# An encoder layer on one core: in the w_down products, weight pieces, adding DMAs, stored sums and x issued at other places

## The chip, the core and the metric

The kernel runs on one core of one Trainium2 chip. The time is device microseconds of that core for one launch. The kernel before takes 2227.09 us (median of three runs, 2224.58 to 2228.4). The profile comes from one further execution, and a kernel's changes are worked out in the times of that execution.

## What is computed

The input is x of 512 tokens by 2048 channels in float32. The layer is

```python
h = rmsnorm(x, attn_norm_w[l]);  proj = h @ w_in[l]      # attention heads and gated linear attention
x = x + concatenate([attn_out, gla_out], axis=-1) @ w_out[l]
h = rmsnorm(x, ffn_norm_w[l])
x = x + (silu(h @ w_gate[l]) * (h @ w_up[l])) @ w_down[l]   # FFN_HIDDEN = 5632
return rmsnorm(x, final_norm_w)
```

The change concerns the last product, with w_down (5632 by 2048).

## The kernel before

The float32 products are made of products of split operands: an operand is split into a rounded part (hi) and what rounding left (lo), and for w_down the products hi\*hi, hi\*lo and lo\*hi are added in PSUM. The large products of the feed-forward part use a seven-product scheme for 2 by 2 blocks (Strassen's, in Winograd's form), so the weights of a block need sums first, then splitting.

The order of the work is written out by hand: each engine (PE for matmuls, ACT and DVE for elementwise work, POOL and SP as issuers of DMAs) gets its instructions in the order in which the Python code records them, and works them off in that order. Buffers are slots: `s4` has 20 slots of 4 KB a partition (tiles named b), `s2` has 62 of 2 KB (tiles named a). A slot is handed out again as soon as the code has put it back; the instruction that then writes it waits on the chip for the last reader.

The product with w_down is done in three parts: four small jobs (`evac_down`), then `Down.run`, then four more jobs and a tail. `Down.run` (L1658) is where the change lies. It works through 64 **pieces**, numbered 0 to 63 here; a piece is one pair of w_down blocks (two row blocks of 128, 512 columns) times one prepared pair of activations, and takes 42 matmuls (L1591, L1592, L1593, three for each half of each of seven products). The pieces form ten **runs**, each the sum over some pairs into seven PSUM banks for one of the four column blocks c:

| run | column block | pieces | what happens at its end |
|---|---|---|---|
| 0, 1, 2 | 0, 1, 2 | 0-5, 6-11, 12-17 | the seven sums are stored in DRAM (`md`, L1614) |
| 3 | 3 | 18-28 | stored (L1614) |
| 4, 5 | 2, 1 | 29-33, 34-38 | added in DRAM to those stored (L1612) |
| 6 | 0 | 39-48 | combined into the result and added to x |
| 7, 8, 9 | 1, 2, 3 | 49-53, 54-58, 59-63 | combined and added to x |

Runs 6 to 9 are the "summed" ones: they begin with the stored sums of the earlier runs. `fetch` (L1555) reads the seven tiles of `md` back into `s2` slots through SP's queue (L1560), and `preload` (L1562) copies each into its PSUM bank on ACT (L1564). A bank is taken by the preload as soon as the run before has read it, so at the last piece of a run ACT has a preload after every evacuation of a bank (L1609 where the run before is stored, L1627 and L1635 where it is combined).

For one piece these steps are needed. SP loads the raw blocks (L1114, 512 KB). DVE makes the sums (`sums`: L1130, L1131, L1132). Then `split` gives hi copies on ACT and lo differences on DVE: in most runs for the raw blocks (128x768) and for the sums (128x1024), L1142 and L1147. In runs 3 and 6, where DVE also prepares activations (`operands`, L1522 to L1538), the lo of the raw blocks is made by `part` (L1474) instead: ACT writes the negative of the raw block rounded (L1481), a DMA issued by POOL adds the raw block to it (L1482, the **adding DMA**), ACT copies the hi (L1483); only the sums are split on ACT and DVE (L1493, L1494). A piece's second matmul, on L1592, is the first that reads the lo of the raw blocks.

In iteration i the code records, ahead of the products of piece i: `sums(i)`, `split(i)`, `sums(i+1)`, `sums(i+2)`, `split(i+1)` and `part(i+2)`; what has been done already is skipped. So while piece i is multiplied, one further piece, i+1, is ready or being made ready. Then come steps of the activations (`make`), the fetch for the next run (in the last piece but one, n = len(part) - 2), and in the second piece of a summed run (n = 1) four loads of x from DRAM by POOL (L1679), which the `residuals` (L1652, on DVE, four of them, two right after a run and two one piece later) add the result to. `combine` (L1618) is the chain of DVE and ACT steps at the end of a summed run (L1621, L1622, L1627, L1635, L1638).

Of the kernel before, what the change touches and what calls it, by code (L numbers as in the profile page):

```python
# [120 lines left out]
def layer(nc, tc, x, attn_norm_w, w_in, rel_table, gw_f, gb_f, gw_b, gb_b, gla_norm_w, w_out,  # L121
# [7 lines left out]
    with tc.manual_schedule(), \  # L129
# [7 lines left out]
        s4 = Slots(p4, N4, 1024, "b")  # L137
# [97 lines left out]
        def run_urgent():  # L235
            while urgent:
                try:
                    next(urgent[0])
                    break
                except StopIteration:  # L240
                    urgent.popleft()
# [911 lines left out]
        class Feed(Blocks):  # L1153
# [183 lines left out]
            def run(self):  # L1337
                for i, (u, q) in enumerate(self.seq):
                    self.load()
                    self.split(i)  # L1340
                    while 2 * q + 1 not in xs:
                        run_urgent()
                    for _ in range((1, 3, 3)[i] if i < 3 else 0):
                        run_urgent()
                    self.sums(i + 1)
                    more = self.sum_steps(i + 2)
                    if q == 0:
                        next(self.making, None)
                    else:
                        next(more, None)  # L1350
                    self.split(i + 1)
                    if i > 3:
                        run_urgent()
                    if q < 3:
                        for _ in more:
                            pass
                        if q < 2:
                            next(self.making, None)
                        self.part(i + 3)
                        if q == 1:  # L1360
                            next(self.making, None)
                    if q == 2 and self.sent:
                        put(self.sent)
                        self.sent = None
                    self.products(i, more)
                    if u == len(self.units) - 1:
                        for p in (2 * q, 2 * q + 1):
                            put(*xs.pop(p).values())
                        down_start(q)
                    if q == self.per - 1:  # L1370
                        self.making = self.combine(u)
                urgent.append(self.last())
# [11 lines left out]
        def g_load(j):  # L1384
            if j < FF // 256 and j not in graw and 2 * j not in gT and j >= state["g"]:
                state["g"] = j + 1
                graw[j] = s4.get(F32, [P, 2, 512])
                sp.dma_start(out=graw[j].t.rearrange("p f t -> p (f t)"), in_=gd[j])

        def g_split(j):  # L1390
            if j in graw:
                r = graw.pop(j)
                for f in (1, 0):
                    hi, lo = s2.get(F32R), s2.get(F32R)
                    if f:
                        act.activation(hi.t, r.t[:, f], AF.Copy, scale=-1.0)
                        dve.scalar_tensor_tensor(lo.t, r.t[:, f], -1.0, hi.f, op0=OP.mult, op1=OP.subtract)
                    else:
                        act.copy(hi.t, r.t[:, f])
                        dve.tensor_tensor(lo.t, r.t[:, f], hi.f, op=OP.subtract)  # L1400
                    gT[2 * j + 1 - f] = (hi, lo)
                put(r)
# [48 lines left out]
        class Down(Blocks):  # L1451
# [206 lines left out]
            def run(self):  # L1658
                for i, (r, q) in enumerate(self.seq):
                    c, part = self.runs[r]  # L1660
                    n = part.index(q)
                    self.load()
                    self.sums(i)
                    self.split(i)
                    self.sums(i + 1)
                    self.sums(i + 2)
                    self.split(i + 1)
                    self.part(i + 2)
                    self.reserve = 11 if r in (4, 5) else 4
                    while q not in self.x:  # L1670
                        self.reserve = 0
                        self.make(1)
                    self.make((r in (3, 6)) + i % 2)
                    if n == len(part) - 2 and r + 1 < len(self.runs) and self.summed(r + 1):
                        self.fetch(r + 1)
                    if self.summed(r) and n == 1:
                        x1[c] = [s2.get() for _ in range(4)]
                        for t in range(4):
                            pool.dma_start(out=x1[c][t].t, in_=xd[4 * c + t])  # L1679
                    self.products(i)  # L1680
                    run_urgent()
                    if r == len(self.runs) - 1:
                        if n == 0:
                            g_load(LAST // 2 - 2)
                        if n == 2:
                            g_split(LAST // 2 - 2)
                            g_load(LAST // 2 - 1)
                            st.until, st.limit = None, 1
                            st.load()
                        if n > 2:  # L1690
                            st.split(later_first + n - 2)
                st.limit, st.big = 3, tail_first
# [142 lines left out]
```

## Time and profile before

| | |
|---|---|
| median of three runs | 2227.09 us |
| the profiled execution | 2224.24 us |
| its span, first to last instruction | 2222.5 us |
| PE busy | 2186.6 us (98%) |
| DVE busy | 1554.6 us (70%) |
| ACT busy | 1201.8 us (54%) |
| POOL busy | 322.5 us (15%) |
| moved by DMA | 373.99 MB, 168 GB/s in the mean |
| `Down.run` on PE | from 1773.96 to 2124.77 us of the span |

Busy PE is not the same as PE at its best: matmuls overlap, and a matmul at the halved clock is just as busy as one at the full clock. What a stage loses is read from its length against its number of matmuls, and from the waits in it.

### The profile page before, as it was taken

Reading aid. Unit: us, or ns where it says so; the run is one execution under the profiler, and the core shown is the slowest. Engines: PE = TensorE matmul, PEld = TensorE weight load, DVE = VectorE, ACT = ScalarE, POOL = GpSimd, SP = SyncE. Lnnn points to the kernel's source line nnn. Section 1 sums busy time; section 2 is a strip of 40 time slices with the busy share of each in tenths; the row PEclk is TensorE's granted clock in tenths of the full one; section 3 lists DMA queues with packets and bytes.
Section 4 is the critical chain, followed back from the end, with each engine's and each line's share of the span. In section 5 each row is a group of like instructions: output and inputs, shape, how many; then the busy total and the mean of one; then the engine's idle time right before and its main releaser. Section 6 shows DMA issues by size and latency. Waiting matters only on the chain.

```text
span 2222.5 us, 33130 instructions
## 1 busy us (share of the span) xinstructions
PE 2186.6 (98%) x12374; PEld 1912.7 (86%) x12374; DVE 1554.6 (70%) x2699; ACT 1201.8 (54%) x2005; POOL 322.5 (15%) x356
## 2 busy tenths in 40 slices
PE   9999999999999999999999999999999999989898
PEld 7888887888888888888888888888888899979886
DVE  4366665745455437888888888888888887868885
ACT  5244444444454346666666666666665656555542
POOL 0000000000000101222222222222222202131000
PEclk9999999999999999999999999999999999999999
DMA  6525625242315325888888888888889857797642
GB/s 207 159 76 146 182 77 147 83 124 61 100 57 187 124 96 128 192 197 204 202 211 196 206 202 198 209 192 214 196 206 212 238 172 225 207 243 215 204 158 76
DMA packets 255457, 373.99 MB, mean 168 GB/s; under 512 B 17951, under 2 KB 179407, under 8 KB 255296
## 3 DMA queue, kind: packets, MB, share of 16 engines
q1 hardware_dynamic: 188768, 252.03, 36.4%
q0 software_dynamic: 65344, 118.80, 27.3%
q8 instruction: 97, 1.59, 0.3%
q10 hardware_dynamic: 1184, 1.06, 0.1%
q14 instruction: 64, 0.52, 0.1%
HBM read 246.58 MB, written 35.19 MB: 127 GB/s over the span
## 4 chain that ended last, share of the span: by engine, by line
PE 92%; DMA 2%; DVE 2%; issue 2%; ACT 1%; POOL 0%; SPq 0%; ACTq 0%; POOLq 0%; DVEq 0%
PE pd L1275 22%; PE pd L1281 11%; PE ps L303 5%; PE ps L304 5%; PE ps L305 5%; PE ps L295 5%; PE ps L297 5%; PE ps L296 5%; PE pe L1275 4%; PE pu L1592 3%; PE pu L1593 3%; PE pu L1591 3%; PE pe L1281 2%; PE ps L529 1%; PE pu L304 1%
## 5 line engine op out<-in xcount | busy, mean ns | idle before, releaser
L1275 PE MATMUL pd<-a,b 128*128 128x512 f32 x2112 | 528.4, 392 | 0.1
L1275 PEld LDWEIGHTS pd<-a,b 128*128 128x128 f32 x2112 | 379.0, 189 | 66.2 <-DVE a L1036 0.5
L1281 PEld LDWEIGHTS pd<-a,b 128*128 128x128 f32 x2112 | 288.5, 190 | 21.5
L1281 PE MATMUL pd<-a,b 128*128 128x256 f32 x2112 | 294.9, 282 | 0.0
L1182 POOL DMA_DIRECT2D b<-b x176 | 209.7, 1248 | 521.6 <-ACT b L1181 393.7
L202 DVE TENSOR_TENSOR a<-b,a 128x512 fp32r<-128x512 f32 x288 | 192.7, 687 | 130.9 <-ACT a L201 130.6
L1220 ACT CAST b<-b 128x1024 fp32r<-128x1024 f32 x176 | 185.4, 1053 | 166.5 <-DVE b L1206 138.5
L1592 PE MATMUL pu<-b,a 128*128 128x256 f32 x896 | 256.6, 286 | 18.5 <-DVE b L1147 9.3
L1591 PE MATMUL pu<-b,a 128*128 128x256 f32 x896 | 256.0, 286 | 2.5 <-ACT pu L1564 2.5
L1593 PE MATMUL pu<-b,a 128*128 128x256 f32 x896 | 255.8, 286 | 0.0
L1221 DVE TENSOR_TENSOR b<-b,b 128x1024 fp32r<-128x1024 f32 x176 | 215.0, 1221 | 50.5 <-ACT b L1220 26.3
L201 ACT CAST a<-b 128x512 fp32r<-128x512 f32 x288 | 169.4, 617 | 48.5 <-PE ps L305 22.3
L1592 PEld LDWEIGHTS pu<-b,a 128*128 128x128 f32 x896 | 174.3, 195 | 20.0 <-DVE b L1147 9.9
L1591 PEld LDWEIGHTS pu<-b,a 128*128 128x128 f32 x896 | 174.3, 195 | 3.1 <-ACT pu L1564 3.1
L1593 PEld LDWEIGHTS pu<-b,a 128*128 128x128 f32 x896 | 174.2, 194 | 0.0
L1303 DVE TENSOR_TENSOR a<-pd,a 128x512 f32<-128x512 f32 x132 | 91.4, 692 | 96.5 <-ACT a L1302 96.5
L1181 ACT ACTIVATE b<-b 128x768 fp32r<-128x768 f32 x176 | 149.4, 849 | 4.7 <-PE ps L305 2.9
L1183 ACT CAST b<-b 128x768 fp32r<-128x768 f32 x176 | 145.5, 827 | 0.6 <-PE ps L305 0.6
L1142 ACT CAST b<-b 128x768 fp32r<-128x768 f32 x86 | 77.0, 941 | 108.9 <-PE pu L1593 104.6
L1302 ACT COPY a<-pd 128x512 f32<-128x512 f32 x132 | 77.6, 588 | 103.0 <-PE pd L1281 103.0
L1203 DVE TENSOR_TENSOR b<-b 128x512 f32<-128x512 f32 x176 | 120.7, 686 | 0.0
L593 ACT CAST b<-ps 128x512 fp32r<-128x512 f32 x64 | 37.6, 587 | 144.8 <-PE ps L529 142.9
(256 smaller groups left out, 4457.4 us busy)
## 6 DMA issues: line engine op xcount, KB each, us to landing
b<-b POOLq DMA_DIRECT2D x197, 384.0 KB, 5.4
b<-in_w_gate_dram SPq DMA_DIRECT2D x88, 512.0 KB, 4.0
b<-in_w_up_dram SPq DMA_DIRECT2D x88, 512.0 KB, 4.5
b<-in_w_down_dram SPq DMA_DIRECT2D x88, 512.0 KB, 5.5
b<-in_w_in_dram SPq DMA_DIRECT2D x48, 512.0 KB, 4.0
b<-in_w_in_dram SPq DMA_DIRECT2D x94, 256.0 KB, 4.3
b<-in_w_out_dram SPq DMA_DIRECT2D x32, 512.0 KB, 4.7
a<-a SPq DMA_DIRECT2D x96, 128.0 KB, 2.4
```

Of the source, the lines that this page charges most:

```text
L201: act.copy(h[2].t, r)
L202: dve.tensor_tensor(h[3].t, r, h[2].f, op=OP.subtract)
L1181: act.activation(lo.t, r, AF.Copy, scale=-1.0)
L1182: pool.dma_start(out=lo.f, in_=r, accum_op=OP.add)
L1183: act.copy(hi.t, r)
L1220: act.copy(hi.t, self.S[i].t)
L1221: dve.tensor_tensor(lo.t, self.S[i].t, hi.f, op=OP.subtract)
L1275: mm(o, wh.t[:, p, k], x_.t.rearrange("p s t -> p (s t)"), start=first and p == 0, stop=False, skip_group_check=True)
L1281: mm(o[:, 256:512], wl.t[:, p, k], x_.t[:, 0], start=False, stop=last and p == 1, skip_group_check=True)
L1591: mm(o, xh[:, t], wh, start=first and not loaded and h == 0, stop=False, skip_group_check=True)
L1592: mm(o, xh[:, t], wl, start=False, stop=False, skip_group_check=True)
L1593: mm(o, xl[:, t], wh, start=False, stop=last, skip_group_check=True)
```

## The change

The products, the sums and the splits stay the same in number and kind; before and after, the order has 11972 rows on PE, 2693 on DVE, 591 on SP and 360 on POOL. What changes is where they are recorded. `part` goes one piece further ahead, to i+3. In the runs that are not 3 or 6, if more than four slots of `s4` are free (more than six in the summed runs), `sums(i+3)` and `split(i+2)` are recorded in iteration i too, so that a second further piece is made ready. With the code's own slot counts this holds in iterations 0-14, 29-35, 51-53, 56-58 and 61-63; it does not hold in 15-17, 36-38, 49, 50, 54, 55, 59 and 60. The fetch moves to the last piece but three, and the loads of x to the last piece but one.

```diff
                     self.sums(i + 1)
                     self.sums(i + 2)
                     self.split(i + 1)
-                    self.part(i + 2)
+                    self.part(i + 3)
+                    if r not in (3, 6) and len(s4.free) > (6 if self.summed(r) else 4):
+                        self.sums(i + 3)
+                        self.split(i + 2)
                     self.reserve = 11 if r in (4, 5) else 4
                     while q not in self.x:
                         self.reserve = 0
                         self.make(1)
                     self.make((r in (3, 6)) + i % 2)
-                    if n == len(part) - 2 and r + 1 < len(self.runs) and self.summed(r + 1):
+                    if n == len(part) - 4 and r + 1 < len(self.runs) and self.summed(r + 1):
                         self.fetch(r + 1)
-                    if self.summed(r) and n == 1:
+                    if self.summed(r) and n == len(part) - 2:
                         x1[c] = [s2.get() for _ in range(4)]
                         for t in range(4):
                             pool.dma_start(out=x1[c][t].t, in_=xd[4 * c + t])
```

The lines below the change stand three further down in the new file (L1679 becomes L1682).

On POOL, at the end of run 5 and the start of run 6, this stood before. The tiles b on the left are the lo of pieces 39, 40, 41, 42 and 43, the md rows are the sums of run 5:

```order
L1482 DMA b_1614_19277<-b_1594_19099 128x768
L1482 DMA b_1620_19348<-b_1600_19162 128x768
L1612 DMA md<-a_1387_19360 128x512
...
L1612 DMA md<-a_1393_19426 128x512
L1482 DMA b_1626_19440<-b_1606_19218 128x768
L1482 DMA b_1633_19516<-b_1612_19274 128x768
L1679 DMA a_1403_19524<-xd 128x512
...
L1679 DMA a_1406_19527<-xd 128x512
L1482 DMA b_1639_19585<-b_1618_19345 128x768
```

And this stands there now:

```order
L1482 DMA b_1608_19235<-b_1594_19036 128x768
L1482 DMA b_1616_19296<-b_1600_19113 128x768
L1482 DMA b_1622_19353<-b_1606_19176 128x768
L1612 DMA md<-a_1387_19365 128x512
...
L1612 DMA md<-a_1393_19431 128x512
L1482 DMA b_1628_19445<-b_1614_19293 128x768
L1482 DMA b_1635_19521<-b_1620_19350 128x768
```

Three adding DMAs (pieces 39, 40, 41) instead of two stand ahead of the seven sums of run 5, and the four loads of x no longer stand between those of pieces 42 and 43.

On DVE, at the end of run 7, this stood before: the lo of piece 54 (L1147), the combine (L1621 and on), two residuals (L1652), the sums and the lo of piece 55 (made from raw block b_1694_20203), two residuals:

```order
L1147 TENSOR_TENSOR b_1710_20389<-b_1688_20145,b_1708_20385 128x768
L1147 TENSOR_TENSOR b_1711_20391<-b_1701_20311,b_1709_20387 128x1024
L1621 TENSOR_TENSOR b_1713_20413<-pu_67_20071,a_1455_20403 128x2x256
...
L1622 TENSOR_TENSOR b_1713_20413<-a_1455_20403,pu_72_20122 128x2x256
L1652 SCALAR_TENSOR_TENSOR a_1444_20205<-b_1713_20413,small,a_1444_20205 128x512
L1652 SCALAR_TENSOR_TENSOR a_1445_20206<-b_1713_20413,small,a_1445_20206 128x512
L1130 TENSOR_TENSOR b_1715_20467<-b_1700_20267 128x512
...
L1147 TENSOR_TENSOR b_1718_20475<-b_1694_20203,b_1716_20471 128x768
L1147 TENSOR_TENSOR b_1719_20477<-b_1707_20381,b_1717_20473 128x1024
L1652 SCALAR_TENSOR_TENSOR a_1446_20207<-b_1714_20453,small,a_1446_20207 128x512
```

And this stands there now:

```order
L1147 TENSOR_TENSOR b_1710_20339<-b_1688_20145,b_1708_20335 128x768
L1147 TENSOR_TENSOR b_1711_20341<-b_1701_20275,b_1709_20337 128x1024
L1130 TENSOR_TENSOR b_1713_20395<-b_1700_20273 128x512
...
L1147 TENSOR_TENSOR b_1716_20403<-b_1694_20203,b_1714_20399 128x768
L1147 TENSOR_TENSOR b_1717_20405<-b_1707_20331,b_1715_20401 128x1024
L1621 TENSOR_TENSOR b_1719_20427<-pu_67_20071,a_1455_20417 128x2x256
...
L1652 SCALAR_TENSOR_TENSOR a_1451_20345<-b_1719_20427,small,a_1451_20345 128x512
L1652 SCALAR_TENSOR_TENSOR a_1452_20346<-b_1719_20427,small,a_1452_20346 128x512
L1652 SCALAR_TENSOR_TENSOR a_1453_20347<-b_1720_20467,small,a_1453_20347 128x512
L1652 SCALAR_TENSOR_TENSOR a_1454_20348<-b_1720_20467,small,a_1454_20348 128x512
L1130 TENSOR_TENSOR b_1721_20525<-b_1706_20287 128x512
```

The sums and lo of piece 55 (again from b_1694_20203) have moved from behind the combine to ahead of it, and the four residuals follow each other with nothing between them.

## The prediction

> **What bounds the kernel now.** The page's chain of work first, then busy time in windows, one for each group of runs of `Down.run`, then single engines where those windows are too long. The chain says that PE sets the end:
>
> ```profile
> PE 92%; DMA 2%; DVE 2%; issue 2%; ACT 1%; POOL 0%; SPq 0%; ACTq 0%; POOLq 0%; DVEq 0%
> ```
>
> The windows are runs 0-2, 3, 4-5, 6, 7, 8 and 9. Look at the length of each and its DMA share (the last column but one):
>
> ```profile
> 1773.96:1864.67 90.71, 90.71 (x757) 90.71 (x756) 73.02 (x106) 47.96 (x68) 13.50 (x23) 1.00 0.58 174
> 1864.67:1921.64 56.97, 55.69 (x464) 55.48 (x463) 47.86 (x85) 38.95 (x59) 12.55 (x19) 1.00 0.95 262
> 1921.64:1972.04 50.40, 50.40 (x422) 50.40 (x421) 36.23 (x49) 25.87 (x36) 9.60 (x13) 1.00 0.71 184
> 1972.04:2035.56 63.52, 53.31 (x422) 52.29 (x421) 41.07 (x72) 38.01 (x58) 16.87 (x23) 0.95 0.97 260
> 2035.56:2066.16 30.60, 27.20 (x213) 26.79 (x211) 25.99 (x37) 14.47 (x20) 2.16 (x4) 0.94 0.56 186
> 2066.16:2096.10 29.94, 26.93 (x212) 26.73 (x211) 25.34 (x36) 14.01 (x19) 2.13 (x4) 0.94 0.56 182
> 2096.10:2124.77 28.67, 25.62 (x213) 25.42 (x212) 23.15 (x35) 14.19 (x20) 2.12 (x4) 1.00 0.81 287
> ```
>
> Runs 0-2 take 90.71/18 = 5.04 us a piece and runs 4-5 take 50.40/10 = 5.04: a piece without waits is 5.04 us. Against that, run 3 (11 pieces) loses 1.53 us, run 6 (10) 13.12, and runs 7, 8, 9 (5 each) 5.40, 4.74 and 3.47. These 28.26 us are all that the change can take away, since the matmuls stay. PE's own waits show where they go:
>
> ```profile
> 1876.31 0.39 PE L1592 MATMUL pu<-b,a 128*128 128x256 f32 x1 [1.28 <-DMA b<-b]
> 1974.44 0.39 PE L1592 MATMUL pu<-b,a 128*128 128x256 f32 x1 [2.12 <-DMA b<-b]
> 1979.40 0.38 PE L1591 MATMUL pu<-b,a 128*128 128x256 f32 x1 [1.23 <-ACT pu L1564]
> 1981.39 0.39 PE L1591 MATMUL pu<-b,a 128*128 128x256 f32 x1 [1.02 <-ACT pu L1564]
> 1993.63 0.58 PE L1592 MATMUL pu<-b,a 128*128 128x256 f32 x1 [5.66 <-DMA b<-b]
> 2044.54 0.39 PE L1592 MATMUL pu<-b,a 128*128 128x256 f32 x1 [3.20 <-DVE b L1147]
> 2074.49 0.39 PE L1592 MATMUL pu<-b,a 128*128 128x256 f32 x1 [3.01 <-DVE b L1147]
> 2104.47 0.39 PE L1592 MATMUL pu<-b,a 128*128 128x256 f32 x1 [3.05 <-DVE b L1147]
> ```
>
> The three waits for `DMA b<-b` are adding DMAs, of pieces 20, 39 and 41; the two for L1564 are banks that piece 39 waited for; the last three are the lo of pieces 50, 55 and 60, the second piece of runs 7, 8 and 9. The waits come to 20.6 us; the rest of the 28.3 is the halved clock behind three of them (0.95, 0.94, 0.94 in the windows) and the pipeline's refill.
>
> **Runs 3 and 6: adding DMAs and the read-back.** At the end of run 5 ACT, SP and POOL show one cause:
>
> ```profile
> 1970.22 0.59 ACT L1564 COPY pu<-a 128x512 f32<-128x512 f32 x1 [0.46 <-DMA a<-md]
> 1970.75 0.58 ACT L1609 COPY a<-pu 128x512 f32<-128x512 f32 x1
> 1971.36 0.59 ACT L1564 COPY pu<-a 128x512 f32<-128x512 f32 x1
> ...
> 1980.75 0.59 ACT L1564 COPY pu<-a 128x512 f32<-128x512 f32 x1 [0.88 <-DMA a<-md]
> 1981.27 0.58 ACT L1609 COPY a<-pu 128x512 f32<-128x512 f32 x1
> 1981.75 1.05 ACT L1493 CAST b<-b 128x1024 fp32r<-128x1024 f32 x1
> 1982.70 0.84 ACT L1481 ACTIVATE b<-b 128x768 fp32r<-128x768 f32 x1
> ```
> ```profile
> 1964.44 4.10 SPq L1560 DMA_DIRECT2D a<-md  x7
> ```
> ```profile
> 1983.84 0.86 POOL L1482 DMA_DIRECT2D b<-b  x1 [0.83 <-ACT b L1481]
> ```
> ```profile
> DMA to landing us min/median/max: 4.3/7.0/10.4
> ```
>
> The fetch is issued at 1964.44, and its last tile is there at 1980.75. ACT stands in that row of preloads; behind them in its order wait the evacuations, the split of piece 40 and the L1481 whose adding DMA piece 41 needs. That DMA goes out at 1983.84 and PE starts on it at 1993.63, 9.8 us later (the last line, of L1482, gives 4.3 to 10.4 for issue to landing). Moved two pieces ahead, the fetch is issued two pieces, 10 us, earlier, and its last tile, 16.3 us behind the issue, is due about 1971, before ACT could use it (below). The weight loads behind it on SP go out 4.1 us later; they are for pieces four and five ahead, 20 us away, so 0. By the Trainium skill (DMA: Bandwidth & Descriptors, Anatomy of one DMA — SWDGE (gpsimd) path) such a DMA takes 2.0 us plus bytes/436e3, an estimate of 2.9 us for 384 KB; by that the earlier `part` would bring nothing, the 1.53 us of run 3 would stay, and the sum below would be 19.7. The trace has three times as much, and the measurement decides.
>
> What is late next: with data there, a preload and an evacuation follow each other in 1.14 us (1970.22 to 1971.36), while PE asks for a bank every 5.04/7 = 0.72 us. Counted from the start of piece 38, ACT has L1493, L1481 and L1483 (2.8 us) ahead of the first preload; the seventh ends at 2.8 + 6 x 1.14 + 0.59 = 10.2, and PE wants it at 5.04 + 6 x 0.72 = 9.4: 0.85 us lost. Then the last evacuation, L1493 and its DVE half (1.2 us) make piece 40 whole at 12.95, needed at 12.4: 0.6. Then L1481 for piece 42 and its DMA, out at 13.8 at the latest; with the 9.8 us of piece 41 it lands at 23.6 less what the queue is now shorter by (the loads of x are gone from it), and PE wants it at 21.7. With the median 7.0 nothing is lost, with 10.4 it is 2.5; I take 0.6. Run 6 keeps 2.05 of 13.12 us, bounds 0 and 4.0; **11.07 saved**.
>
> Piece 20 waited 1.28 us for a DMA that was issued behind seven stores of run 2. It is now recorded one piece (5.04 us) earlier, ahead of them; piece 21 takes its place behind them with 5.04 - 1.28 = 3.8 us to spare. **1.53 saved**. The adding DMAs of steady pieces did not hold PE up and get 5 us more.
>
> **Runs 7 to 9: DVE.** The rows of DVE, and three of ACT, from the end of run 6 and of run 7:
>
> ```profile
> 2034.70 0.69 DVE L1621 TENSOR_TENSOR b<-pu,a 128x512 f32<-128x512 f32 x1 [2.35 <-ACT a L1627]
> ...
> 2040.68 1.42 DVE L1652 SCALAR_TENSOR_TENSOR a<-b,small,a 128x512 f32<-128x512 f32 x2
> 2042.01 0.69 DVE L1130 TENSOR_TENSOR b<-b 128x512 f32<-128x512 f32 x1
> ...
> 2043.54 2.08 DVE L1147 TENSOR_TENSOR b<-b,b 128x768 fp32r<-128x768 f32 x2
> ```
> ```profile
> 2033.57 0.59 ACT L1564 COPY pu<-a 128x512 f32<-128x512 f32 x1 [2.47 <-DMA a<-md]
> ...
> 2061.32 1.79 ACT L1142 CAST b<-b 128x768 fp32r<-128x768 f32 x2 [3.25 <-PE pu L1593]
> ...
> 2068.84 1.19 ACT L1564 COPY pu<-a 128x512 f32<-128x512 f32 x2 [0.94 <-DVE a L1638]
> ```
> ```profile
> 2062.18 2.18 DVE L1147 TENSOR_TENSOR b<-b,b 128x768 fp32r<-128x768 f32 x2 [1.21 <-ACT b L1142]
> 2064.65 0.69 DVE L1621 TENSOR_TENSOR b<-pu,a 128x512 f32<-128x512 f32 x1 [0.28 <-ACT a L1627]
> ...
> 2069.91 0.68 DVE L1622 TENSOR_TENSOR b<-a,pu 128x512 f32<-128x512 f32 x1
> ```
> ```profile
> L1621 DVE TENSOR_TENSOR a<-a,a 128x512 f32<-128x512 f32 x1 | 0.7, 693 | 1.2 <-ACT a L1635 1.2
> ```
>
> Piece 50: its lo comes behind the combine of run 6 and two residuals, and that order stays (in iterations 48 and 49 nothing more is recorded ahead). But the combine began late because ACT waited 2.47 us for a stored sum, now read two pieces earlier. The run's last piece began at 2035.56 - 5.04 = 2030.52, its second bank is whole 1.6 us later, and L1621 can start about 2032.4 instead of 2034.70. Everything behind it comes 2.3 us earlier, but PE's clock for piece 49 also loses its 0.46 us of bank waits: of the wait of 3.20 about 1.5 stays, of the 4.93 us around it (halved clock included; waits up to 2.12 us, and in run 9 even 3.05, left the clock whole) 3.4 goes. With 0.46 and 0.2 given back at piece 51, **3.7 of 5.40 saved**, bounds 1.5 and 5.4.
>
> Pieces 55 and 60 get their lo ahead of the combine, so 4.74 and 3.47 go. But DVE has little to spare: in run 7 it is busy 25.99 us, and idle 0.3 + 1.2 inside the combine, against PE's 25.2. The set of one more piece (sums 1.5, lo 2.1 = 3.6 us) now has to fit ahead of the combine. From L1621 at 2032.4 DVE works without a pause through combine (5.9, from 2064.65 to 2070.6), four residuals (2.8) and the sets of pieces 50 to 55 (6 x 3.6 = 21.6): 2062.7. PE begins the run's last piece at 2030.52 + 25.2 + 1.7 (the waits left at 50 and 51) = 2057.4. So the combine starts 5.3 us after that piece's start, where it now starts 3.5 after it (2064.65 against 2066.16 - 5.04), 1.8 us later, and the preloads that follow its steps too. The sixth of them ended at 2068.84 + 0.59 = 2069.4, and PE wanted its bank at 2066.16 + 5 x 0.72 = 2069.8: 0.3 us in hand. That makes about 1.6 us of bank waits at piece 54, and the same at piece 59. So **3.1 of 4.74 and 1.8 of 3.47 saved**; bounds for the two together 2 (waits of 3 us at both, each with a halved clock) and 8.2.
>
> Loads of x: POOL has nothing else by then, and the residuals need x some 12 us after the new place; 0, and at worst a DMA's 10.4 us, still inside. Runs 0-2, 4, 5: the extra set is made while DVE has idle time (73.02 of 90.71 busy); 0.
>
> **Sum.** 1.53 + 11.07 + 3.7 + 3.1 + 1.8 = 21.2 us. The profiled execution is 2224.24 us, 1.7 over its span of 2222.5; it would be 2203.0. It stood 2.85 below the median of the runs, 2227.09, which becomes **2205.9 us**.
>
> **Rivals.** *All waits go* (0.13): DVE's backlog and the banks cost nothing; 2227.1 - 28.3 = 2198.8 us. For it: each remaining wait above is a difference of about 1 us between long chains. Against: DVE's 25.99 + 1.5 exceeds 25.2.
>
> *DMA becomes the bound in run 6* (0.20). Its share there is 0.97 of 63.52 us, or 61.6 us. Out of the window go about five of the seven reads (1.3 MB at 260 GB/s, 5 us) and one adding DMA (1.5 us); about half of run 7's read-back comes in (3.5 us). That leaves 58.6 us where I count 52.5: 6.1 us less gain, 2212 us. For it: nothing is taken off the queues in total. Against: a window half empty lies on either side (0.71, 0.56).
>
> *Slower* (0.04). ACT works in order, and the second set's hi copies wait for PE to leave a slot. If they wait longer than today's, the evacuations and preloads behind them start a piece late at the five run ends with a second set (0, 1, 4, 7, 8): 5.04 us and 1.7 for the halved clock (4.74 - 3.01 in run 8) each, 34 us, less the 21 saved: 2240 us. It decides from the moment that the copies are released later than the run's last piece begins. For it speaks the Trainium skill too (TensorE: Matmul & The Clock Gate, Architectural detail): ACT and DVE are strict FIFOs. Against: 2061.32 shows today's copy released when the last piece begins, and the set that frees the new copy's slots is the same one.
>
> *No change* (0.03): banks and DVE give back everything.
>
> **How the numbers follow.** Forecast 0.60, its own range 2202 to 2210. Low end 2199.5, at the first rival; high end 2216, past the DMA rival. A run of this kernel tells apart about 0.2%, 4.5 us: faster 0.93, same 0.03, slower 0.04.
>
> **What would show it.** Right: no PE wait for `DMA b<-b` at pieces 20, 39, 41; no ACT wait for `DMA a<-md`; no wait for L1147 at 55 and 60, one of 1 to 2 us at 50; short waits for L1564 in pieces 39, 54, 59; granted clock 1.00 in all windows. Wrong: waits of over 3 us for `DMA b<-b` at 42 to 44 (the DMA rival), or any wait in runs 0-2, 4 or 5.

## The result, and the profile after

| | before | after |
|---|---|---|
| median (4 runs each, same chip) | 2225.98 us (2224.58 to 2228.4) | 2204.56 us (2203.45 to 2205.03) |
| profiled execution, its span | 2224.24, 2222.5 us | 2204.33, 2202.6 us |
| `Down.run` on PE | 350.81 us | 329.98 us (1774.89 to 2104.86) |

The ratio is 0.9902 (95%: 0.9885 to 0.9919): 21.4 us faster in the medians, 1.3 us below the forecast of 2205.9 and inside its range. `Down.run` is 20.83 us shorter. It begins 0.93 us later than before, behind code that all kernels here share (it begins between 1773.3 and 1775.3 us in the 14 traces); what follows it is as long as it was. The profile counts otherwise than the rows of the order, but alike in both kernels (12374 matmuls on PE, 2699 instructions on DVE, 2005 on ACT): the work is the same.

The chain of work that ended last, from the page of after, now has less of DMA, DVE and issue in it:

```profile
PE 94%; DVE 3%; ACT 1%; issue 1%; DMA 1%; POOL 0%; SPq 0%; ACTq 0%; POOLq 0%; DVEq 0%
```

The windows of after over runs 0-2, 3, 4-5, 6, 7, 8 and 9 (start and end, length, busy PE, PEld, DVE, ACT, POOL with their instructions, granted clock, DMA share, GB/s):

```profile
1774.88:1865.60 90.72, 90.72 (x758) 90.71 (x756) 72.22 (x106) 49.48 (x71) 14.41 (x24) 1.00 0.64 188
1865.60:1921.04 55.44, 55.44 (x465) 55.44 (x463) 48.06 (x85) 37.07 (x57) 11.09 (x17) 1.00 0.89 241
1921.04:1971.44 50.40, 50.40 (x423) 50.40 (x421) 35.95 (x50) 27.93 (x39) 11.48 (x15) 1.00 0.83 231
1971.44:2023.78 52.34, 51.52 (x422) 50.62 (x421) 41.51 (x72) 37.33 (x57) 15.49 (x21) 1.00 1.03 288
2023.78:2051.14 27.36, 25.46 (x213) 25.26 (x211) 26.62 (x39) 14.12 (x19) 1.61 (x3) 1.00 0.53 181
2051.14:2077.95 26.81, 26.03 (x212) 25.40 (x211) 24.90 (x37) 14.12 (x19) 1.61 (x3) 1.00 0.62 198
2077.95:2104.86 26.91, 26.20 (x213) 25.57 (x212) 21.11 (x32) 13.22 (x19) 3.19 (x6) 1.00 0.74 246
```

Run 3 lost 1.53 us and loses nothing now. Run 6 went from 63.52 to 52.34, run 7 from 30.60 to 27.36, run 8 from 29.94 to 26.81, run 9 from 28.67 to 26.91. The clock is 1.00 in every window, where it was 0.94 and 0.95 in runs 6 to 8. But the DMA share of run 6 is now 1.03: the records of the 16 DMA engines add up to more than the window, so some of them overlap and little idle time can be left. That will matter below.

PE's waits inside `Down.run` in after, grouped (sum in us, times, longest):

```profile
PE pu L1592 <- DVE b L1147: 1.9, 1, 1.9
PE pu L1591 <- ACT pu L1564: 1.8, 6, 0.6
...
PE pu L1592 <- DMA b<-b: 0.3, 1, 0.3
PE pu L1592 <- DVE b L1494: 0.2, 1, 0.2
```

The long waits of before, 1.28, 2.12 and 5.66 us for an adding DMA and three of over 3 us for L1147, have shrunk to one of 1.9, and the rest are of 0.6 us at most.

At the end of run 5, the rows of SP and of ACT in after:

```profile
1953.79 4.72 SPq L1560 DMA_DIRECT2D a<-md  x7
```
```profile
1969.02 0.58 ACT L1564 COPY pu<-a 128x512 f32<-128x512 f32 x1
1969.54 0.58 ACT L1609 COPY a<-pu 128x512 f32<-128x512 f32 x1
1970.15 0.59 ACT L1564 COPY pu<-a 128x512 f32<-128x512 f32 x1
...
1976.37 0.58 ACT L1609 COPY a<-pu 128x512 f32<-128x512 f32 x1
1976.84 1.05 ACT L1493 CAST b<-b 128x1024 fp32r<-128x1024 f32 x1
1977.79 0.85 ACT L1481 ACTIVATE b<-b 128x768 fp32r<-128x768 f32 x1
```

The read-back starts 15.2 us ahead of the first preload, not 5.8, and no preload carries a releaser any more: seven pairs follow each other in 1.13 to 1.14 us (1969.02, 1970.15). Then comes the L1481 of piece 42, at 1977.79.

DVE, from the end of run 6 to the end of run 7 in after:

```profile
2019.09 2.17 DVE L1147 TENSOR_TENSOR b<-b,b 128x768 fp32r<-128x768 f32 x2 [1.91 <-ACT b L1142]
2021.18 0.68 DVE L1621 TENSOR_TENSOR b<-pu,a 128x512 f32<-128x512 f32 x1
...
2023.83 0.69 DVE L1621 TENSOR_TENSOR a<-a,a 128x512 f32<-128x512 f32 x1 [1.17 <-ACT a L1635]
...
2027.14 1.42 DVE L1652 SCALAR_TENSOR_TENSOR a<-b,small,a 128x512 f32<-128x512 f32 x2
...
2030.00 2.09 DVE L1147 TENSOR_TENSOR b<-b,b 128x768 fp32r<-128x768 f32 x2
...
2051.44 0.68 DVE L1621 TENSOR_TENSOR b<-pu,a 128x512 f32<-128x512 f32 x1
```

The lo of piece 50 is the L1147 of 2030.00. It stands behind the combine (from 2021.18), two residuals and the sums of piece 51, and PE waits 1.9 us for it. From 2021.18 to the next combine at 2051.44 DVE rests only inside the combine, 1.17 us.

### The profile page after: what moved, and what is told of

Same layout as the page of the kernel before. It is cut to its first block, busy times and chain, and to the rows that moved or that the text cites. A ratio compares the mean times of both kernels' runs of the same rounds, so it can differ in the third digit from the quotient of the medians.

```text
span 2202.6 us, 33125 instructions
## 1 busy us (share of the span) xinstructions
PE 2183.5 (99%) x12374; PEld 1908.7 (87%) x12374; DVE 1552.0 (70%) x2699; ACT 1201.6 (55%) x2005; POOL 322.5 (15%) x356
## 4 chain that ended last, share of the span: by engine, by line
PE 94%; DVE 3%; ACT 1%; issue 1%; DMA 1%; POOL 0%; SPq 0%; ACTq 0%; POOLq 0%; DVEq 0%
PE pd L1275 22%; PE pd L1281 11%; PE ps L303 5%; PE ps L295 5%; PE ps L305 5%; PE ps L304 5%; PE ps L296 5%; PE ps L297 5%; PE pu L1592 4%; PE pu L1591 4%; PE pu L1593 4%; PE pe L1275 4%; PE pe L1281 2%; PE ps L529 1%; PE pu L304 1%; PE pu L305 1%
## 5 line engine op out<-in xcount | busy, mean ns | idle before, releaser
L1591 PEld LDWEIGHTS pu<-b,a 128*128 128x128 f32 x896 | 171.9, 192 | 3.5 <-ACT pu L1564 3.5
L1592 PEld LDWEIGHTS pu<-b,a 128*128 128x128 f32 x896 | 171.9, 192 | 3.1 <-DVE b L1147 2.1
L1593 PEld LDWEIGHTS pu<-b,a 128*128 128x128 f32 x896 | 171.9, 192 | 0.0
```

The source lines that it names most:

```text
L1591: mm(o, xh[:, t], wh, start=first and not loaded and h == 0, stop=False, skip_group_check=True)
L1592: mm(o, xh[:, t], wl, start=False, stop=False, skip_group_check=True)
L1593: mm(o, xl[:, t], wh, start=False, stop=last, skip_group_check=True)
```

## The experiments

The loss of a piece is the time from its first matmul to the first of the next piece, less 5.04 us. All kernels in one table, in us, from the profiled execution of each ("other" has pieces 38, 48, 53, 58 and 63). The medians are of all executions, and the profiled one can lie off them: it took 2220.32 us in e2, 2216.84 in e5, 2211.97 in e6 and 2213.5 in e12, each 2 to 4 us above the median, so the losses in these rows are those of a longer execution.

| kernel | 20 | 39 | 40 | 41 | 42 | 49 | 50 | 54 | 55 | 59 | 60 | other | sum | median, us | ratio to before (95%) |
|---|---|---|---|---|---|---|---|---|---|---|---|---|---|---|---|
| before | 1.53 | 5.13 | 0.44 | 7.55 | | 0.46 | 4.93 | | 4.75 | | 3.31 | 0.16 | 28.3 | 2225.98 | |
| after | | 0.82 | 0.45 | 0.13 | 0.55 | | 2.15 | 1.61 | | 1.55 | | 0.16 | 7.4 | 2204.56 | 0.9902 (0.9885-0.9919) |
| e1_part | | 5.80 | 1.07 | | 0.88 | | 2.17 | | 4.90 | | 3.43 | 0.16 | 18.4 | 2214.56 | 0.9949 (0.9935-0.9964) |
| e2_fetch | 1.72 | 0.87 | 0.45 | 9.73 | | | 1.43 | | 4.37 | | 4.37 | 0.24 | 23.2 | 2216.94 | 0.9956 (0.9939-0.9973) |
| e3_second | 0.21 | | 0.19 | 9.17 | | 0.86 | 4.95 | 2.33 | | 1.81 | | 2.11 | 21.6 | 2217.26 | 0.9959 (0.9944-0.9974) |
| e4_xlate | 1.32 | 4.62 | 0.44 | 7.73 | | 1.80 | 4.95 | | 4.87 | | 3.27 | 2.28 | 31.3 | 2227.45 | 1.001 (1.000-1.0019) |
| e5_no_second | | 2.61 | 0.45 | 0.14 | 3.81 | | 3.65 | | 4.37 | | 5.53 | 0.45 | 21.0 | 2214.12 | 0.995 (0.9935-0.9965) |
| e6_no_part | 0.33 | | 0.19 | 9.29 | | | 1.47 | 1.64 | | 1.57 | | 0.16 | 14.6 | 2209.93 | 0.9928 (0.9911-0.9944) |
| e7_no_fetch | | 1.70 | 0.43 | 0.15 | 5.63 | | 3.66 | 2.35 | | 1.80 | | 2.19 | 17.9 | 2214.52 | 0.995 (0.9935-0.9965) |
| e8_x_early | | 0.83 | 0.44 | 0.14 | 1.22 | | 3.66 | 0.32 | | 1.55 | | 0.16 | 8.3 | 2204.91 | 0.9906 (0.9891-0.9921) |
| e9_dma_lo | | 0.82 | 0.45 | 0.13 | 0.81 | | 1.63 | 1.82 | 2.28 | 1.67 | 3.76 | 0.65 | 14.0 | 2209.69 | 0.9928 (0.9913-0.9943) |
| e11_evac_dve | | | | | 4.99 | | 3.64 | 0.30 | | 1.57 | | 0.16 | 10.7 | 2205.77 | 0.9912 (0.9897-0.9926) |
| e10_both | | | | | 4.78 | | 1.63 | 1.51 | 2.28 | 0.63 | 3.78 | 0.16 | 14.8 | 2210.57 | 0.9933 (0.9917-0.995) |
| e12_act_resid | | 0.82 | 0.43 | 0.15 | 1.28 | 0.43 | 0.96 | 4.90 | | 5.76 | | 0.16 | 14.9 | 2209.89 | 0.9933 (0.9919-0.9947) |

Each kernel stands beside a median of before from the same chip, and these lie between 2225.29 and 2225.98 us; after was timed on one chip alone, so a difference to after of less than 1 us says nothing.

### One part alone: e1 to e4

The kernel before with `part` one piece further ahead:

```diff
-                    self.part(i + 2)
+                    self.part(i + 3)
```

> Only the adding DMAs are one piece earlier (part(i+3)); everything else is as before. My theory: the wait at piece 20 goes (1.5 us); piece 39 still waits for its banks, since ACT still stands before the stored sums until about 1981, but piece 41's DMA now goes out ahead of that, so its 7.5 us go and piece 42 waits about 1 us: 8 us faster than before, 2218 us. Rival, the read-back alone holds run 6: only the 1.5 us of run 3 go, 2224.5 us.

It took 2214.56 us, 10.7 less than before. The 7.55 us of piece 41 are gone: its adding DMA now leaves ahead of the seven sums. Piece 39 still loses 5.80, and ACT's waits in this kernel, from 1960 to 2000 us, say why:

```profile
ACT pu L1564 <- DMA a<-md: 4.6, 5, 1.8
```

The stored sums are still read late and the preloads wait for them. Not expected was that piece 50 fell to 2.17, without a change to DVE's order or to the place of the fetch. SP's reads at the end of run 6 in this kernel, and then in before:

```profile
2016.19 4.41 SPq L1560 DMA_DIRECT2D a<-md  x7
```
```profile
2026.57 5.64 SPq L1560 DMA_DIRECT2D a<-md  x7
```

Piece 48 begins at 2023.44 here and at 2030.52 in before: the reads go out 7.25 us ahead of it instead of 3.95. SP works in order, and the reads stand behind loads of raw blocks, which wait for slots; with run 6 less held up by late adding DMAs, those loads go out sooner against PE. That last link is read from the rows of SP, and no run tests it alone.

The kernel before with the fetch two pieces earlier:

```diff
-                    if n == len(part) - 2 and r + 1 < len(self.runs) and self.summed(r + 1):
+                    if n == len(part) - 4 and r + 1 < len(self.runs) and self.summed(r + 1):
```

> Only the stored sums are read back two pieces earlier. My theory: ACT has no waits for md; piece 39's bank waits shrink to under 1 us, but piece 41's adding DMA still goes out behind ACT's run-end copies and piece 41 waits some 6 us with the halved clock; piece 50's wait shrinks from 3.2 to about 1.7 us: 6 us faster, 2220 us. Rival, the late read-back is the single cause in run 6: 11 us of run 6 and 3.7 of run 7 go, 2211 us.

It took 2216.94 us, 8.4 less. Piece 39 falls to 0.87 and piece 50 to 1.43, as the read-back is there in time at both run ends. But piece 41 goes from 7.55 to 9.73: PE comes to it earlier, its adding DMA still stands behind the seven sums, and the wait is 6.77 us instead of 5.66.

The kernel before with the second ready piece alone:

```diff
                     self.part(i + 2)
+                    if r not in (3, 6) and len(s4.free) > (6 if self.summed(r) else 4):
+                        self.sums(i + 3)
+                        self.split(i + 2)
```

> Only the second ready piece; adding DMAs, read-back and x as before. My theory: the waits for the lo of pieces 55 and 60 go (8.2 us) and bank waits of 1.6 us come at pieces 54 and 59: 5 us faster, 2221 us. Rival, DVE has time to spare: 8.2 us faster, 2217.8 us, no bank waits. Rival, the wait only moves: no change, 2226 us.

It took 2217.26 us, 8.0 less. Pieces 55 and 60 lose nothing, and 54 and 59 get bank waits in their place, as forecast. What was not forecast is piece 39, which loses nothing although the fetch is where it was. SP's row in this kernel:

```profile
1958.55 3.69 SPq L1560 DMA_DIRECT2D a<-md  x7
```

The same seven reads go out 5.9 us earlier than before (1964.44), again behind loads on SP: by the order of the code the second ready set lets go of raw slots earlier, so that the loads go earlier and the reads with them. Piece 20 falls from 1.53 to 0.21 as well, so this part does nearly the same there as the earlier `part` does in e1.

The kernel before with x loaded late:

```diff
-                    if self.summed(r) and n == 1:
+                    if self.summed(r) and n == len(part) - 2:
```

> Only the loads of x late in a run. My theory: nothing waits for x and what the loads held up in run 6 is set by something else: no change, 2226 us within 2. Rival, DMA is the bound in run 6: the 1 MB of x leaves the crowded stretch, some 4 us at 260 GB/s, piece 41 waits about 2 instead of 5.7 us: 2221 us.

It took 2227.45 us, 2.2 more than before (interval 0 to 0.19%, so hardly clear of the noise). The loss is at one place, the end of run 6, where pieces 48 and 49 lose 2.1 and 1.8 (before: 0 and 0.46). The first preload of ACT there, and the time from issue to landing of the reads (L1560 from 2015 to 2040 us, first in this kernel, then in before):

```profile
2036.29 0.59 ACT L1564 COPY pu<-a 128x512 f32<-128x512 f32 x1 [5.94 <-DMA a<-md]
...
DMA to landing us min/median/max: 9.3/9.9/10.1
```
```profile
DMA to landing us min/median/max: 5.4/7.2/7.4
```

The preload waits 5.94 us instead of 2.47: the x tiles and the reads are on the DMA engines at once.

The four gains alone are 10.7 + 8.4 + 8.0 - 2.2 = 24.9 us; together they bring 21.4. They overlap: e2 and e3 both bring the first read-back forward, e1 and e3 both free piece 20, e1 and e2 both shorten piece 50.

### One part undone: e5 to e8

The kernel after without the second ready piece, the three lines of e3 taken out:

```diff
-                    if r not in (3, 6) and len(s4.free) > (6 if self.summed(r) else 4):
-                        self.sums(i + 3)
-                        self.split(i + 2)
```

> The changed kernel without the second ready piece. My theory: pieces 55 and 60 wait 3 us each for their lo again, with halved clocks, and the bank waits at 54 and 59 (1.6 and 1.5 us) go; the read-back is early by itself, so run 6 starts as in the changed kernel: 5 to 6 us slower than it, 2210 us. Rival, the second piece pays by letting the raw loads and the read-back behind them on SP go earlier: with the fetch moved anyway nothing is left of that, 2205 to 2206 us.

It took 2214.12 us, 9.6 above after. Pieces 55 and 60 lose 4.37 and 5.53 again (54 and 59 nothing); but in the profiled execution pieces 39, 42 and 50 lose 6.6 us more than in after, which was not expected (1.5 of it, at piece 50, is the halved clock that the last section is about). On ACT the L1481 of piece 41 waits for its raw block, and the preloads start 4.7 us into piece 38 instead of 2.6:

```profile
1968.52 0.84 ACT L1481 ACTIVATE b<-b 128x768 fp32r<-128x768 f32 x1 [1.93 <-DMA b<-in_w_down_dram]
```

So the second set is worth something in run 6 too, where it isn't used: through raw slots, it seems, as in e3.

The kernel after with `part` at i+2 again:

```diff
-                    self.part(i + 3)
+                    self.part(i + 2)
```

> The changed kernel with the adding DMAs two pieces ahead, as before. My theory: piece 41's DMA goes out behind ACT's run-end copies and piece 41 waits 6 to 7 us, with a halved clock after it, some 9 us in all against the 0.7 us that pieces 41 and 42 lose in the changed kernel: 2213 us. Rival, DMA is the bound of run 6 and the order does not matter: the same loss shows elsewhere in run 6 with both, 2205 us.

It took 2209.93 us, 5.4 above after. All of the loss is piece 41: 9.29 us, a wait of 6.74 for its adding DMA and the halved clock behind it:

```profile
PE pu L1592 <- DMA b<-b: 6.7, 1, 6.7
```

Pieces 39 and 40 lose 0 and 0.19, where after loses 0.82 and 0.45: with one `part` less ahead of them ACT starts the preloads earlier.

The kernel after with the fetch in the last piece but one again:

```diff
-                    if n == len(part) - 4 and r + 1 < len(self.runs) and self.summed(r + 1):
+                    if n == len(part) - 2 and r + 1 < len(self.runs) and self.summed(r + 1):
```

> The changed kernel with the read-back in the last piece but one, as before. My theory after the single parts: the second piece brings the read-back of run 6 forward by 5 us on SP, so run 6 starts well; at the ends of runs 6, 7 and 8 ACT waits for stored sums, 4 us lost at pieces 48 and 49 (where the loads of x now fall too) and 1 to 2 us more at 54 and 59: 2211 us. Rival, the read-back place is what matters in run 6: piece 39 loses 4 us as before and piece 40, 41 follow, 2215 us or more.

It took 2214.52 us, 10.0 above after, more than expected. The 4 us expected at pieces 48 and 49 did not come; at the ends of runs 7 and 8 ACT waits for stored sums, and pieces 53, 54, 58 and 59 lose 6.2 us where after loses 3.2. At the start of run 6 piece 42 waits 3.89 us for an adding DMA. SP's reads and the window of run 6 in this kernel:

```profile
1962.39 4.70 SPq L1560 DMA_DIRECT2D a<-md  x7
```
```profile
1970.80:2029.12 58.32, 53.60 (x423) 52.27 (x421) 41.77 (x72) 37.72 (x57) 15.51 (x21) 0.97 1.01 280
```

The reads go out 8.6 us later than in after (1953.79), 8.4 us ahead of run 6, and take 6.1 to 8.3 us each from issue to landing, so that the later ones land in run 6. Its share is 1.01 in 58.32 us, 58.9 us of the engines' time where after needs 53.9: what after has done in run 5 now adds to a queue that is full.

The kernel after with x loaded in the second piece again:

```diff
-                    if self.summed(r) and n == len(part) - 2:
+                    if self.summed(r) and n == 1:
```

> The changed kernel with x loaded in the second piece of a run, as before. Theory that DMA is nearly the bound at the start of run 6 (share 1.03 there): 1 MB of x at 260 GB/s, some 4 us, comes between the adding DMAs of pieces 42 and 43, which wait 1 to 3 us longer: 2206 to 2208 us. Rival, the place of x costs and gives nothing: 2204.6 us.

It took 2204.91 us, which can't be told from after. The late loads of x bring nothing and cost nothing once the other three parts are in. Piece 42 waits 0.96 us for its adding DMA instead of 0.30, with the four loads on the engines beside it; for the rest the two differ at pieces 50 and 54 alone, by the halved clock that the last section is about.

### What is left: e9, e11, e10, e12

Four kernels take up what after still loses. First, less work for DVE in runs 7 to 9, where the lo of the raw blocks goes to ACT and adding DMAs; the second set isn't made there:

```diff
-                return i < self.n and self.seq[i][0] in (3, 6)
+                return i < self.n and self.seq[i][0] in (3, 6, 7, 8, 9)
...
-                    if r not in (3, 6) and len(s4.free) > (6 if self.summed(r) else 4):
+                    if r not in (3, 6, 7, 8, 9) and len(s4.free) > (6 if self.summed(r) else 4):
```

> The kernel after, with the lo of the raw blocks made by ACT and an adding DMA (part) in runs 7, 8 and 9 too, and so without the second ready set there (part takes its place, three pieces ahead). Theory, that what is left at pieces 50, 54 and 59 is DVE's work: DVE loses about 1 us for each of 15 pieces (the L1147 of the raw block), so that its backlog behind the combine goes; the wait of 1.9 us for L1147 at piece 50 falls to 0.5 or less, the bank waits at 54 and 59 go, -3 to -5 us, 2200 to 2201.5 us, with a DMA share in runs 7 to 9 that rises from 0.53 to 0.74 to some 0.6 to 0.8. Rival, that the adding DMAs meet the read-back and the weight loads there as in run 6: waits for DMA b<-b at pieces 50 to 52, 55 and 60, no gain or a loss, 2204 to 2212 us.

It took 2209.69 us, 5.1 above after. Runs 7, 8 and 9 of this kernel in windows, and then one row each of ACT and DVE at the end of run 8:

```profile
2022.61:2049.93 27.32, 25.61 (x212) 25.21 (x210) 19.31 (x29) 15.59 (x22) 6.49 (x9) 1.00 0.93 263
2049.93:2079.23 29.30, 26.40 (x211) 25.57 (x211) 20.68 (x31) 17.85 (x25) 6.50 (x9) 1.00 0.87 248
2079.23:2110.02 30.79, 27.95 (x213) 27.12 (x212) 21.15 (x32) 15.78 (x23) 6.03 (x10) 0.94 0.90 282
```
```profile
2076.97 0.84 ACT L1481 ACTIVATE b<-b 128x768 fp32r<-128x768 f32 x1 [2.21 <-DMA b<-in_w_down_dram]
```
```profile
2079.57 0.69 DVE L1621 TENSOR_TENSOR b<-pu,a 128x512 f32<-128x512 f32 x1 [3.55 <-ACT a L1627]
```

DVE's load fell from 26.62 to 19.31 us in run 7, and the waits at 54 and 59 stayed. The combine starts 0.34 us after run 9 begins (2079.57 against 2079.23), as in after at run 8 (2051.44 against 2051.14), but now DVE waits for ACT, and ACT waited for a raw block, with the DMA share at 0.87 to 0.93 instead of 0.53 to 0.74. Neither theory had this: at these places there is no wait for the adding DMAs themselves, but one for a load beside them. And since the second set was left out, the lo of the sums of pieces 55 and 60 comes behind the combine again, with 2.02 us of wait each. That is most of what e9 loses: 2.28 and 3.76 us at these two pieces, of 6.6 in the sum. This kernel thus changes two things at once and does not show what taking DVE's work away alone would do.

Second, run 5's banks copied by DVE, which has time there, instead of ACT:

```diff
-                act.copy(y.t, bank.t)
+                dve.tensor_copy(y.t, bank.t) if (c, n) in self.seen and c == 1 else act.copy(y.t, bank.t)
```

> The kernel after, with the copies of run 5's seven banks into s2 on DVE instead of ACT. Theory, that pieces 39 and 40 are late because a preload and an evacuation on ACT take 1.14 us for a bank that PE wants every 0.72 us: with the evacuation on DVE (about 0.7 us) beside the preload (0.59 us) on ACT the banks keep up, the 0.82 us at piece 39 and the 0.45 at piece 40 go, and ACT reaches the L1481 of piece 42 earlier, so that its 0.55 goes too: -1.3 to -1.8 us, about 2203 us. Rival, that these waits come from the seven transfers of run 5's sums or from the read-back: no change, 2204.5 us, with the same waits for L1564.

It took 2205.77 us, no better than after. The first half of the theory holds: the seven preloads take 4.10 us in one row, and pieces 39 to 41 lose nothing. But piece 42 loses 4.99 us. The rows of ACT and POOL, and PE's wait:

```profile
1968.64 4.10 ACT L1564 COPY pu<-a 128x512 f32<-128x512 f32 x7
```
```profile
1975.23 1.27 POOL L1482 DMA_DIRECT2D b<-b  x1
```
```profile
PE pu L1592 <- DMA b<-b: 3.3, 1, 3.3
```

Counted from the start of run 6 (1971.07 here, 1971.44 in after), the adding DMA of piece 42 is issued 4.2 us in instead of 7.5 (1978.93 in after), and PE starts on it 18.7 us in (1989.72) instead of 17.1 (1988.54). The landing of the adding DMAs between 1965 and 1990 us, in after and then here:

```profile
DMA to landing us min/median/max: 6.2/8.3/9.6
```
```profile
DMA to landing us min/median/max: 6.3/12.1/14.4
```

So counted, that of piece 42 is issued 3.3 us earlier and is there 1.6 us later: it takes 14.4 us to land instead of 9.6. PE comes to piece 42 1.4 us earlier, and the two make the wait of 3.25 us out of 0.30, with the halved clock on top. The stores of run 5's sums now stand closer together ahead of this DMA, and SP's next loads go out 3.8 us earlier beside it (1975.40 instead of 1979.18); which of the two delays it, no run tells apart.

Both edits in one:

> Both edits of the last two kernels in one. By the theory their gains are at different places and add up: -4 to -6.5 us, 2198 to 2200.5 us. By the rival of the first (adding DMAs in runs 7 to 9 run into the read-backs) 2203 to 2211 us.

It took 2210.57 us. Run 6 is that of e11 (piece 42: 4.78), runs 7 to 9 nearly those of e9. The losses stand side by side and nothing is gained; the rival's range holds it, though not by the waits that the rival named.

Third, the residuals of runs 6 to 8 off DVE:

```diff
-                    dve.scalar_tensor_tensor(x1[c][t].t, y[t // 2].t[:, t % 2], rstd2[:, t:t + 1], x1[c][t].t,
-                                             op0=OP.mult, op1=OP.add)
+                    f = y[t // 2].t[:, t % 2]
+                    if c < 3:
+                        act.activation(f, f, AF.Copy, scale=rstd2[:, t:t + 1])
+                        pool.dma_start(out=x1[c][t].t, in_=f, accum_op=OP.add)
+                    else:
+                        dve.scalar_tensor_tensor(x1[c][t].t, f, rstd2[:, t:t + 1], x1[c][t].t,
+                                                 op0=OP.mult, op1=OP.add)
```

> The kernel after, with the residuals of runs 6, 7 and 8 (L1652, four a run, 2.74 us of DVE together) taken off DVE: ACT multiplies the result by its scale in place (0.6 us each) and a DMA adds it to the x tile. Theory, that what is left at pieces 50, 54 and 59 is DVE's total: in the kernel after, DVE works from the start of run 6's combine to the start of run 7's without a pause but one inside the combine (5.9 + 2.7 + 6 x 3.6 = 30.2 us, and 2021.18 to 2051.44 is 30.26). With 2.74 less the combine of run 7 starts in time, so the bank waits at pieces 54 and 59 go (1.61 and 1.55 us); at piece 50 ACT's two multiplications stand ahead of the hi copy instead, so that the wait falls only from 1.9 to about 1.0. -2.5 to -4 us, 2200.5 to 2202 us. Rival, that ACT takes DVE's place as it did when the lo was moved to it in runs 7 to 9 (ACT waits for the combine's last step, and the copies and preloads behind it start as late as now): the same waits at 50, 54 and 59, no change or up to 2 us slower, 2204.5 to 2206.5 us.

It took 2209.89 us, 5.3 above after. The profiled execution took 2213.5, and what follows `Down.run` is 2.3 us longer in it than in after. At piece 50 the theory holds: the waits are 0.27 and 0.61 us, 0.88 where 1.0 was expected and after has 1.9. Then DVE, ahead of its time at last, runs out of raw blocks. Rows of DVE in this kernel, and a window of 20 us of it:

```profile
2044.08 0.69 DVE L1130 TENSOR_TENSOR b<-b 128x512 f32<-128x512 f32 x1 [1.59 <-DMA b<-in_w_down_dram]
...
2050.04 0.69 DVE L1130 TENSOR_TENSOR b<-b 128x512 f32<-128x512 f32 x1 [2.34 <-DMA b<-in_w_down_dram]
...
2053.57 0.68 DVE L1621 TENSOR_TENSOR b<-pu,a 128x512 f32<-128x512 f32 x1
```
```profile
2032.00:2052.00 20.00, 20.00 (x168) 19.91 (x166) 15.65 (x24) 9.83 (x13) 3.12 (x6) 1.00 0.97 309
```

The combine starts at 2053.57, 3.06 us after run 8 began (2050.51), and pieces 54 and 59 lose 4.90 and 5.76 instead of 1.61 and 1.55. In those 20 us the DMA engines are busy to 0.97. The adding DMAs into x, the loads of x that stand behind them on POOL (from 2032.36), the raw blocks and the read-back all fall into them, and a raw block (issued from 2033 to 2056 us) takes up to 9.9 us to land where after has 5.7 at most. Which of these delays the raw blocks most, no run tells apart. Neither the theory's time nor the rival's mechanism came out: ACT was in time, the loads were not.

No kernel of these beats after. e11 and e12 each take away a wait that is there (at pieces 39 and 40, and at 50) and give it back, and more, at the DMA queues; e9, and e10 with it, loses most by the second set that it leaves out.

## Why the prediction was right, point by point

**The bound and the whole.** The 28.26 us of waits were the right place, and nothing else moved. The sum was 21.2 us; `Down.run` gave 20.8, the medians 21.4. That not all waits would go was right too: 7.4 us stayed.

**Run 3.** 1.53 forecast, 1.53 measured. The reason given, an earlier `part`, is one of two: e1 without the second set loses nothing at piece 20, e3 without the earlier `part` 0.21.

**Run 6.** 2.05 us were to stay, 1.95 did: 0.82, 0.45, 0.13 and 0.55 at pieces 39 to 42, where 0.85, 0.6 and 0.6 were worked out for 39, 40 and 42. e1, e2 and e6 show its two links apart: with the read-back late (e1: ACT waits 4.6 us for `md`) run 6 loses 7.8 us, with the adding DMA late (e2 and e6: piece 41 waits 6.77 and 6.74) 11.1 and 9.5. A third link is missing from the prediction, which put the second set at nothing outside runs 7 to 9: without it (e5) run 6 loses 7.0 us, and with it alone (e3) the read-back already goes out 5.9 us earlier. So the number for run 6 holds for the four parts together, and not for the two parts that it was credited to. e11 shows the pair of 1.14 us on ACT as the cause at pieces 39 and 40, which lose nothing there.

**The price of an adding DMA.** In after those of runs 3 and 6 take this long (L1482 from 1865 to 2024 us):

```profile
DMA to landing us min/median/max: 5.7/7.5/9.6
```

The Trainium skill (DMA: Bandwidth & Descriptors, Anatomy of one DMA — SWDGE (gpsimd) path) gives a fit by which 384 KB take 2.9 us, an estimate, by which the prediction had the earlier `part` bring nothing. The measurement decides against it: beside other traffic the median is 7.5 us, and the earlier `part` alone (e1) brings 10.7 us.

**DMA in run 6.** This rival was given 0.20 and 2212 us. It was wrong in size and right in kind. The queue was to need 58.6 us; it needed 1.03 of 52.34, or 53.9. More of the traffic than counted moved ahead: runs 4 and 5 went from a share of 0.71 to 0.83 of 50.40 us, 6.0 us, and run 6 moved 15.1 MB instead of 16.5 (its GB/s times its length). And each us of the engines' time moved a little more, 0.28 MB instead of 0.27. So PE waits only 0.30 us for it. But it lies right at PE's heels: e7 and e11 lose at once, 3.89 and 3.25 us of wait at piece 42, when something is put back into the queue or PE comes sooner.

**Run 7.** This is the term that was sized worst: 1.7 us were to stay (1.5 at piece 50, 0.2 at 51), 2.16 did. The order is as forecast, combine, residuals, sums, lo. The step that failed is the start of the combine, put at 1.9 us after the run's last piece began, when its second bank is whole. It starts 2.44 us after it (2021.18 against 2018.74), because DVE is busy until then with the lo of piece 49, which had waited 1.91 us for the hi copies on ACT. That is 0.54 us, against 0.46 of miss. That the wait of 1.9 us left the clock whole is luck: in e5, e7, e8 and e11 the same wait costs 3.64 to 3.66 us instead of 2.15.

**Runs 8 and 9.** The combine was to start 5.3 us after the last piece's start; it does 5.34 after (2051.44 against 2046.10). 1.6 us were to be lost to bank waits at each of pieces 54 and 59; they lose 1.61 and 1.55. This is DVE's total for the run, not its order: in e8 and e11, where piece 50 lost 1.5 us more, piece 54 lost 1.3 less. So the luck at piece 50 is worth only some 0.2 us over the two pieces there.

**x.** Costed at nothing; e8 bears it out in the whole. Alone it cost 2.2 us (e4), by a collision with the read-back that the prediction did not name; the earlier fetch takes it out of the way.

**The slower rival** (copies of the second set held up on ACT): no wait of that kind at the run ends of after, and the gains at pieces 55 and 60 came (e3, e5).

## What to carry to other kernels

Read, for each place where the bound engine waits, the whole chain behind the wait: here three waits of one line had three different causes (a read-back, a DMA behind stores, an engine's order), and each had its own cure. A queue worked off in order ties buffers to transfers: a step that frees slots earlier can bring a read-back 5.9 us forward without touching it, so measure each part alone and undone before you credit it. And when the waits are gone, look at what is nearly full (here the DMA engines, 1.03 in run 6 and 0.97 in e12's window): what e11 and e12 saved on ACT and DVE was paid back there.

## What the runs showed of the hardware that was not expected

The prediction took it as a bare fact that waits of up to 2.12 us, and one of 3.05, left the clock whole, while others of 3 us halved it. With all traces together this has a rule. The clock records of a run lie on a grid of 3.413 us. In one such stretch PE of after stands still for 1.74 us (3.42 less 1.68 busy), PE of e5 for 1.90, at the same wait of 1.90 us at piece 50. The windows on that grid, of after and then of e5 (granted clock is the third column from the right):

```profile
2029.26:2032.68 3.42, 1.68 (x14) 1.68 (x15) 3.39 (x6) 1.64 (x2) 0.00 (x0) 1.00 0.28 102
2032.68:2036.09 3.41, 3.41 (x31) 3.41 (x30) 3.34 (x7) 0.00 (x0) 0.00 (x0) 1.00 0.30 112
```
```profile
2032.22:2035.63 3.41, 1.51 (x13) 1.30 (x12) 3.34 (x6) 2.17 (x3) 0.00 (x0) 1.00 0.27 77
2035.63:2039.04 3.41, 3.41 (x19) 3.41 (x18) 3.34 (x6) 0.00 (x0) 0.00 (x0) 0.50 0.50 159
```

In the one the boundary cuts the wait and the clock stays 1.00; in the other the whole wait lies in one stretch and the next one runs at 0.50, which costs some 1.5 us. The wait of 3.05 us in before (piece 60) is cut nearly in half:

```profile
2099.79:2103.20 3.41, 1.63 (x14) 1.43 (x12) 3.31 (x7) 2.66 (x4) 2.12 (x4) 1.00 0.81 267
2103.20:2106.62 3.42, 2.15 (x18) 2.15 (x19) 3.42 (x5) 1.05 (x1) 0.00 (x0) 1.00 0.73 244
```

Over the `Down.run` of all 14 traces there are 68 stretches at full clock with over 0.8 us of stillness, summed from the gaps between matmuls: in 39 of them, with 0.87 to 1.78 us, the next stretch is at full clock; in 29, with 1.88 to 3.41 us, it is at half. So a little over half of a stretch is the limit, and whether one wait of 1.9 to 3.2 us costs its own length or some 1.5 us more depends on where it falls (3.17 us in e1 at piece 60 left the clock whole, 3.20 in before at piece 50 did not). That is luck: a difference of 1.5 us between two kernels at such a wait (piece 50 in e5, e7, e8 and e11 against e1 and after) says nothing of the edit. The Trainium skill (TensorE: Matmul & The Clock Gate, Part 1: The HAM clock gate) tells of a free-running window of 3413 ns, which these traces show as the grid of 3.413 us. The Trainium skill (TensorE: Matmul & The Clock Gate, HAM oscillation — how this bites in real kernels) also gives a rule of no idle gaps over some 3.4 us; here 1.88 us in one window were enough.
